# Sample rows turned as whole 128-row tiles, and retention keys in a zero-padded page

## The chip, the cores and the metric

One Trainium2 chip, one of its cores. The metric is device time in microseconds (us) of one execution of the program; lower is better. The engines are TensorE (PE; its weight loads are shown as PEld), VectorE (DVE), ScalarE (ACT), GpSimd (POOL) and the DMA queues that SyncE (SP) issues.

## The reference

Two layers of a hybrid encoder. In each layer every row of x is normalised and projected by `w_in`; three groups of heads work side by side (four retention heads, eight latent-attention heads, four chunk-band heads); their gated outputs are joined and projected by `w_out` onto the residual. It is done for a prompt of 1024 rows and for a sample of 32 rows that have a past (a retention state, 128 cached latent keys, 128 cached band keys). Of the parts that matter here:

```python
def _retention_block(q, k, v, S):               # per head h, dk = dv = 64
    inner = einsum('blhd,bmhd->bhlm', q, k) * dmask
    o = einsum('bhlm,bmhe->blhe', inner, v) + einsum('blhd,bhde->blhe', q, S) * xi
    S_new = gamma ** L * S + einsum('blhd,blhe->bhde', k * zeta, v)
def _dense_attn(q, k, v, bias):                 # the 32 sample rows, against 128 + 32 keys
    return softmax(q k^T * d ** -0.5 + bias) v
```

## The kernel before

The rows are nine tiles: t = 0 to 7 are 128 prompt rows each, t = 8 holds the 32 sample rows (`n = NS`). A projection needs rows turned (features on the partitions), and so do the keys and queries of every score product. A turn is `tr` (line 185, L187 in the trace): a transpose on TensorE against the top left corner of an identity as large as the input has rows, so a tile of 32 rows is turned by a 32x32 identity. All other products go through `mm` (line 180, L181 in the trace). A product of two plain fp32 operands is two MATMUL records in the trace; a turn, and a product of fp32r operands (the split hi and lo parts of projections and latent scores), is one. A MATMUL's form is read as contraction rows * output rows, so `64*128` uses 64 rows of the array and `32*96 32x32` is a turn of 32 rows into 96.

`layer_in` runs the projections in chunks of columns (`pj` banks), a tile at a time, and spawns tasks from their callbacks: `b_task` (latent attention, with `q_task` and `kv_task`), `band_k_task` and `band_task`, `ret_task` (retention), `mla_sample` and `band_sample` for the sample. A task is a generator; a poll between pieces of a projection steps those that are ready. `NEED` and `MOST` say how many of the 60 pages (SBUF tiles of 128x512 fp32) a kind of task may still need, and a task is stepped only if they are free. A scheduler orders the recorded instructions on each engine; each engine then runs its own in that order. After `layer_in` come latent attention over the prompt (`mla`) and the output projections (`out_part`).

`ret_task` (line 928), once per tile and layer: rotate q and k on POOL and DVE, giving `rz` with q heads 0 to 3 and k heads 0 to 3; turn it in four turns of two heads each (`s<-ident,rz`) into one PSUM bank; ACT copies that to `rT`. Each 128-partition slab of `rT` holds two heads, one on partitions 0 to 63 and one on 64 to 127. So the scores are products over 64 partitions each (`s<-rT 64*128`), those of the first and of the second head of a pair into two PSUM banks. Then the state's update (`s<-zk,rz`), decay on DVE (`inn`), the output (`s<-zk,inn` and `s<-S,rT`), its norm, and two turns of the result (`s<-ident,roc`). The PSUM banks of `ret_task` have the tag "s" (three banks), those of the sample attention the tag "ps" (three).

The turns of the sample's 32 rows are `ps<-ident,z` (in `b_task`, line 609, and in `band_sample`), `ps<-ident,kt` and `ps<-ident,zq` (in `mla_sample`, eight in a row for each half of the heads), `ps<-ident,bqs` (`band_sample`), `s<-ident,rz` and `s<-ident,roc` (`ret_task`) and `s<-ident,yres` (`prep`, between the layers). Attention over values works on 64 output rows (`ps<-P,sv 128*64`, `ps<-bs,bv 128*64`) and stays as it is.

Of the kernel before, what the change touches and what calls it, by code (L numbers as in the profile page):

```python
# [20 lines left out]
NS = 32  # L21
# [37 lines left out]
NEED = dict(prep=2, misc=2, b=8, ret=4, bk=2, bq=7, band=14, smp=3, mla=4)  # L59
MOST = dict(prep=1, misc=2, b=4, ret=2, bk=1, bq=7, band=7, smp=3, mla=4)  # L60
# [42 lines left out]
class Kern:  # L103
# [356 lines left out]
    def prep(self, t, xh, hT):  # L460
# [17 lines left out]
        for j in range(2):  # L478
            p = self.bank((4, 128), "prep")
            for i in range(4):  # L480
                self.tr(p[:, i, :n], xn[j][:n, 128 * i:128 * i + 128])
            self.parts(t, j, p[:, :, :n], hT)
# [82 lines left out]
    def unload(self, t, p, W, z=None, raw=False):  # L565

        if z is None:
            z = self.page([W], name="z")
        with self.urgent(URGENT_Z):
# [11 lines left out]
    def b_task(self, l, t, z, raw):  # L581
# [26 lines left out]
        for i in range(3):  # L608
            self.tr(p[:, i, :n], bn[:n, 128 * i:128 * i + 128])
# [64 lines left out]
    def q_task(self, l, t, n, ch, cl):  # L674
        for c in range(2):
            p = self.bank((4, 96), "b")
            self.latent(p, ch, cl, [(k, self.W["u"][2 * k + c]) for k in range(2)])
            zq = self.page([4, 96], name="zq")
            self.unstack(zq[:n], p)
# [25 lines left out]
    def kv_task(self, l, t, n, ch, cl, kr):  # L705
# [3 lines left out]
        for c in range(2):  # L709
            p = self.bank((4, 128), "b")  # L710
            self.latent(p, ch, cl, [(2, self.W["u"][4 + c])])
            kt = self.page([4, 96], name="kt")
            zk = kt[:, :, :64]
# [43 lines left out]
    def mla_sample(self, l):  # L757
        s = self.bank((2, 160))
        for c in range(2):
# [168 lines left out]
    def ret_task(self, l, t, zk, zq):  # L928
# [3 lines left out]
        z = self.page([2, 4, 2, 32], name="rz")  # L932
        tmp = self.page([2, 4, 2, 32], name="rt")
# [66 lines left out]
        oc = self.page([4, 64], name="roc")  # L1000
        self.act(oc[:n], o[:n])
# [8 lines left out]
        for i in range(2):  # L1010
            self.tr(p[:, i, :n], oc[:n, 2 * i:2 * i + 2].rearrange("p h d -> p (h d)"))
# [264 lines left out]
    def band_sample(self, l, zq, r):  # L1276
        A = self.A
        qn = self.page([4, 64], name="bqs")
        self.tt(qn[:NS], zq, r[:NS].unsqueeze(2).to_broadcast([NS, 4, 64]), OP.mult)
# [4 lines left out]
        p = self.bank((2, 192))  # L1284
        for i in range(2):
            self.tr(p[:, i, :128], kc[:, 128 * i:128 * i + 128])
            self.tr(p[:, i, 128:160], self.bks[:NS, 2 * i:2 * i + 2].rearrange("p h d -> p (h d)"))
            self.tr(p[:, i, 160:192], qn[:NS, 2 * i:2 * i + 2].rearrange("p h d -> p (h d)"))
# [3 lines left out]
        self.act(qT, p[:, :, 160:], scale=self.cols[:, 4:5])  # L1292
# [130 lines left out]
    def out_part(self, l, pairs, x_of, y_of, y_cb=None, eng="D", halves=False):  # L1423
# [10 lines left out]
        def ahead(t, cs):  # L1434
# [3 lines left out]
            for c in cs:  # L1438
                ys[c] = self.page([512], name="yres")
                self.load(ys[c][:n], x_of(t)[:, 512 * c:512 * c + 512])  # L1440
# [31 lines left out]
    def layer_in(self, l, hT):  # L1472
# [35 lines left out]
        def cb_ck(t, p):  # L1508
            self.spawn("bk", self.band_k_task(l, t, self.unload(t, p, 256)))
# [187 lines left out]
```

## Time and profile before

| | us |
|---|---|
| median of 3 runs | 1370.53 |
| lowest and highest of them | 1366.14 and 1373.83 |
| the profiled execution | 1364.83 |
| its span (first to last instruction) | 1363.0 |
| PE busy in it | 1313.6 |
| PEld, DVE, ACT, POOL busy | 1204.4, 847.6, 767.0, 462.8 |
| granted TensorE clock, mean | 0.996 |

The span is cut by stage at about 200, 320, 400, 700, 880, 1000 and 1070 us: projections of layer 0, retention with gates (200 to 320), band attention (to 400), latent attention and output (to 700), and the same again for layer 1. PE's busy time counts a MATMUL from its start to its modelled end, some 0.27 us for a small one, while the next may start 0.11 us later; so what a MATMUL costs on PE is read from the distance of starts, not from its length.

### The profile page before, as it was taken

The page shows a single profiled execution, that of the slowest core. Times are in us where ns is not written, and L with a number is a line of the kernel's source. Part 1 is how long each engine was busy: PE and PEld are TensorE (multiplying, and loading weights), DVE is VectorE, ACT ScalarE, POOL GpSimd, SP SyncE. Part 2 cuts the span into 40 slices and gives each one's busy share as a digit, 9 for nine tenths or more (in the row PEclk, how much of TensorE's full clock was granted, in tenths as well). Part 3 has the DMA queues.
Part 4 walks back from the last instruction along what each step waited for, and adds up shares of the span by engine and source line. Part 5 has one row for each costly group of instructions (what it writes and reads, how often), then busy time and mean ns, then how long its engine had stood idle before and what let it go on. Part 6 is the DMA issues. An engine that isn't in the chain of part 4 may idle for free.

```text
span 1363.0 us, 27760 instructions
## 1 busy us (share of the span) xinstructions
PE 1313.6 (96%) x9883; PEld 1204.4 (88%) x9883; DVE 847.6 (62%) x2568; ACT 767.0 (56%) x2177; POOL 462.8 (34%) x686
## 2 busy tenths in 40 slices
PE   7899999999999999989999999999999999999898
PEld 6799999999898888877889999989999988888786
DVE  7656666666768656656563565675675675665543
ACT  7555463355548667666663554533554585775641
POOL 4666766332002113120323576773310031312210
PEclk9899999999999999999999999999999999999999
DMA  7353430121104433233331534301221152333231
GB/s 249 101 159 101 132 110 17 47 84 48 55 24 115 133 119 111 91 97 109 128 118 34 153 111 130 94 23 47 77 67 41 40 162 87 125 96 120 80 127 66
DMA packets 131074, 130.51 MB, mean 96 GB/s; under 512 B 14392, under 2 KB 107256, under 8 KB 130936
## 3 DMA queue, kind: packets, MB, share of 16 engines
q1 hardware_dynamic: 130360, 127.69, 30.3%
q8 instruction: 78, 1.28, 0.4%
q10 hardware_dynamic: 576, 1.05, 0.2%
q14 instruction: 60, 0.49, 0.1%
HBM read 84.48 MB, written 45.79 MB: 96 GB/s over the span
## 4 chain that ended last, share of the span: by engine, by line
PE 75%; DMA 5%; POOL 5%; DVE 5%; ACT 4%; issue 2%; SPq 0%; ACTq 0%; DVEq 0%; POOLq 0%
PE pj L181 42%; PE s L181 12%; PE ps L181 9%; PE ps L187 8%; POOL rs L246 3%; PE pj L187 2%; DMA raw<-in_w_in 1%; PE s L187 1%; ACT P L191 1%; DVE st L218 1%; DMA qd<-zq 1%; DMA kd<-kt 1%; ACT whi L191 1%; POOL ms L207 1%; DMA raw<-in_w_out 1%
## 5 line engine op out<-in xcount | busy, mean ns | idle before, releaser
L181 PE MATMUL pj<-whi,H 128*128 128x256 f32 (+1 forms) x1792 | 369.2, 297 | 11.0 <-ACT H L191 6.8
L181 PEld LDWEIGHTS pj<-whi,H 128*128 128x128 f32 x1792 | 293.1, 191 | 16.6 <-ACT H L191 7.1
L181 PE MATMUL pj<-wlo,H 128*128 128x256 f32 (+1 forms) x896 | 264.6, 296 | 0.6 <-DVE wlo L214 0.6
L181 PE MATMUL pj<-H,whi 128*128 128x384 f32 (+1 forms) x768 | 192.0, 329 | 0.1
L181 PEld LDWEIGHTS pj<-wlo,H 128*128 128x128 f32 x896 | 171.3, 191 | 3.0 <-DVE wlo L214 1.0
L246 POOL TENSOR_TENSOR rs<-ms,nhalf 128x4 f32<-128x4 f32 (+4 forms) x141 | 166.7, 1183 | 8.8
L199 POOL TENSOR_TENSOR mlo<-mix,mhi 128x256 fp32r<-128x256 f32 x96 | 68.9, 738 | 290.6 <-ACT mhi L191 183.1
L181 PE MATMUL s<-H 96*128 96x384 f32 (+3 forms) x576 | 140.2, 360 | 9.9 <-ACT P L191 9.9
L199 POOL TENSOR_TENSOR wlo<-raw,whi 128x512 fp32r<-128x512 f32 x32 | 41.3, 1295 | 272.5 <-ACT whi L191 159.6
L181 PEld LDWEIGHTS pj<-H,whi 128*128 128x128 f32 x768 | 132.6, 188 | 1.0 <-issue 0.6
L218 DVE TENSOR_REDUCE st<-s 128x1 f32<-128x384 f32 (+3 forms) x240 | 128.0, 535 | 7.3 <-PE s L181 4.5
L191 ACT ACTIVATE P<-ps 128x384 f32<-128x384 f32 (+2 forms) x192 | 89.2, 488 | 73.1 <-PE ps L187 72.1
L181 PE MATMUL pj<-H,wlo 128*128 128x384 f32 (+1 forms) x384 | 125.4, 328 | 0.0
L207 POOL TENSOR_SCALAR ms<-st 128x4 f32<-128x4 f32 (+6 forms) x166 | 58.3, 351 | 194.6 <-DVE st L218 166.0
L191 ACT ACTIVATE P<-s,st 128x384 f32<-128x384 f32 (+2 forms) x192 | 110.1, 580 | 20.9 <-DVE st L207 18.4
L191 ACT ACTIVATE whi<-raw,cols 128x256 fp32r<-128x256 f32 (+2 forms) x182 | 85.5, 517 | 62.0 <-DMA raw<-in_w_in 44.5
L214 DVE SCALAR_TENSOR_TENSOR wlo<-raw,cols,whi 128x256 fp32r<-128x256 f32 (+2 forms) x184 | 88.7, 515 | 38.4 <-ACT whi L191 27.4
L181 PEld LDWEIGHTS s<-H 96*128 96x128 f32 x576 | 93.1, 189 | 20.9 <-ACT P L191 13.3
L181 PE MATMUL pj<-whi,mhi 128*128 128x512 f32 x256 | 102.8, 401 | 1.0 <-ACT mhi L191 0.4
L181 PE MATMUL pj<-wlo,mhi 128*128 128x512 f32 x256 | 101.1, 395 | 0.0
L181 PE MATMUL pj<-whi,mlo 128*128 128x512 f32 x256 | 100.5, 394 | 0.0
L187 PE MATMUL ps<-ident,P 128*128 128x128 f32 x576 | 87.3, 273 | 6.5 <-ACT P L191 6.5
(253 smaller groups left out, 2809.6 us busy)
## 6 DMA issues: line engine op xcount, KB each, us to landing
raw<-in_w_in SPq DMA_DIRECT2D x80, 256.0 KB, 2.9
raw<-in_w_out SPq DMA_DIRECT2D x32, 256.0 KB, 3.0
yp<-yres SPq DMA_DIRECT2D x32, 256.0 KB, 2.0
yres<-yp SPq DMA_DIRECT2D x32, 256.0 KB, 3.0
qd<-zq SPq DMA_DIRECT2D x32, 192.0 KB, 1.9
kd<-kt SPq DMA_DIRECT2D x32, 192.0 KB, 2.3
bd<-z SPq DMA_DIRECT2D x48, 128.0 KB, 1.8
sk<-kd SPq DMA_DIRECT2D x32, 192.0 KB, 2.6
```

The lines of the kernel that those rows point to most:

```text
L181: self.nc.tensor.matmul(out, lhsT, rhs, start=start, stop=stop)
L187: self.nc.tensor.transpose(out, in_, self.ident[:k, :k])
L191: r = self.nc.scalar.activation(out, in_, func, **kw)
L199: (self.nc.vector if eng == "D" else self.nc.gpsimd).tensor_tensor(out, a, b, op=op)
L207: (self.nc.vector if eng == "D" else self.nc.gpsimd).tensor_scalar(out, a, s1, s2, op0=op0, **kw)
L214: self.nc.vector.scalar_tensor_tensor(out, a, s, b, op0=op0, op1=op1)
L218: self.nc.vector.tensor_reduce(out, in_, axis=AX.X, op=op, negate=negate)
L246: self.nc.gpsimd.tensor_tensor(r[:n], ms[:n], self.nhalf[:n, :w], op=OP.pow)
```

## The change

1. Each turn of a sample tile now takes the whole page of 128 rows and the whole 128x128 identity. Rows 32 to 127 of that page have to be zeros, so the page is set to zero on POOL before the 32 rows are written (`z`, `zq`, `kt`, `rz`, `roc`, `bqs`, `yres`, and `z` of the band's keys). Consumers still read 32 columns of the result. `mla_sample` and `band_sample` use a bank of their own for the turned q.
2. In `ret_task`, for all nine tiles: `rT` keeps the q slabs only; the turned keys go to a new page `kz`, zeroed on POOL, in two ACT copies, one head's 64 partitions into the first half and the other's into the second. The score products then contract over all 128 partitions (zeros meet the other head's queries), and all four land in one PSUM bank instead of two.
3. `NEED` and `MOST` of retention go from 4 and 2 pages to 5 and 3.

```diff
-NEED = dict(prep=2, misc=2, b=8, ret=4, bk=2, bq=7, band=14, smp=3, mla=4)
-MOST = dict(prep=1, misc=2, b=4, ret=2, bk=1, bq=7, band=7, smp=3, mla=4)
+NEED = dict(prep=2, misc=2, b=8, ret=5, bk=2, bq=7, band=14, smp=3, mla=4)
+MOST = dict(prep=1, misc=2, b=4, ret=3, bk=1, bq=7, band=7, smp=3, mla=4)
...
     def unload(self, t, p, W, z=None, raw=False):
...
             z = self.page([W], name="z")
+            if t == 8 and raw:
+                self.memset(z, 0.0, "G")
...
     def mla_sample(self, l):
...
-            p = self.bank((2, 4, 32))
+            p = self.bank((4, 128))
             for i in range(4):
-                self.tr(p[:96, 0, i], self.ks[0][c][:NS, i])
-                self.tr(p[:96, 1, i], self.qs[c][:NS, i])
+                self.tr(p[:96, i], self.ks[0][c][:, i])
             for j in range(2):
-                self.act(kT[j][:96, :, 128:], p[:96, 0, 2 * j:2 * j + 2], scale=self.cols[:96, 1:2])
-            self.act(qT[:96], p[:96, 1], scale=self.cols[:96, 0:1])
+                self.act(kT[j][:96, :, 128:], p[:96, 2 * j:2 * j + 2, :NS], scale=self.cols[:96, 1:2])
+            p = self.bank((4, 128))
+            for i in range(4):
+                self.tr(p[:96, i], self.qs[c][:, i])
+            self.act(qT[:96], p[:96, :, :NS], scale=self.cols[:96, 0:1])
...
     def ret_task(self, l, t, zk, zq):
...
         z = self.page([2, 4, 2, 32], name="rz")
+        if t == 8:
+            self.memset(z, 0.0, "G")
...
         p = self.bank((4, 128), "ret")
         for i in range(4):
-            self.tr(p[:, i, :n], rx[:n, 2 * i:2 * i + 2].rearrange("p h d -> p (h d)"))
-        rT = self.page([4, 128], name="rT")
-        self.act(rT[:, :, :n], p[:, :, :n])
-        yield
-        s = [self.bank((2, n), "ret") for _ in range(2)]
+            self.tr(p[:, i], rx[:, 2 * i:2 * i + 2].rearrange("p h d -> p (h d)"))
+        rT = self.page([2, 128], name="rT")
+        kz = self.page([2, 2, 128], name="kz")
+        self.memset(kz, 0.0, "G")
+        self.act(rT[:, :, :n], p[:, :2, :n])
         for i in range(2):
             r = slice(64 * i, 64 * i + 64)
+            self.act(kz[r, i, :, :n], p[r, 2:, :n])
+        yield
+        s = self.bank((2, 2, n), "ret")
+        for i in range(2):
             for pr in range(2):
-                self.mm(s[i][:n, pr], rT[r, 2 + pr, :n], rT[r, pr, :n], True, True)
+                self.mm(s[:n, i, pr], kz[:, i, pr, :n], rT[:, pr, :n], True, True)
+        self.free(kz)
...
-                self.stt(inn[:n, i, pr], s[i][:n, pr], GAM[2 * pr + i] ** -n, self.tri[:n, :n], OP.mult, OP.mult)
+                self.stt(inn[:n, i, pr], s[:n, i, pr], GAM[2 * pr + i] ** -n, self.tri[:n, :n], OP.mult, OP.mult)
```

The other turns (in `prep`, `b_task`, the result's turn in `ret_task`, `band_sample`) change in the same way, each with its memset where the page isn't zeroed already.

The built programs have 8774 products and turns each. Three places of PE's order follow; `pj` are projections, which fill the space between tasks.

First, PE at the retention scores of the fourth tile of layer 0. Before:

```order
L181 MATMUL pj_3658<-H_94,wlo_3319 128x288
L181 MATMUL pj_3658<-H_94,whi_3318 128x288
L181 MATMUL pj_3658<-H_95,whi_3318 128x288
L181 MATMUL s_3668<-rT_3633 128x128 x2
L181 MATMUL s_3669<-rT_3633 128x128 x2
L181 MATMUL s_3674<-zk_2261,rz_3520 128x128 x2
L181 MATMUL pj_3658<-H_94,wlo_3319 128x288
```

With the change:

```order
L181 MATMUL pj_3679<-H_94,whi_3260 128x288
L181 MATMUL pj_3679<-H_95,whi_3260 128x288
L181 MATMUL s_3689<-rT_3623,kz_3624 128x128 x4
L181 MATMUL s_3694<-zk_2263,rz_3501 128x128 x2
L187 MATMUL s_3702<-ident,rz_3587 128x128 x4
L181 MATMUL pj_3679<-H_94,wlo_3261 128x288
```

The four score products stand together as before, now with `kz` as an operand and one bank, and the next tile's turns follow at once.

Second, PE in layer 1 at the first half of the latent sample's turns (`kt` 96x128 of cached keys, then keys and queries of the 32 rows). Before:

```order
L181 MATMUL pj_12459<-wlo_12185,H_94 128x256
L181 MATMUL pj_12459<-whi_12184,H_95 128x256
L187 MATMUL ps_12512<-ident,kt_12251 96x128 x4
L187 MATMUL ps_12519<-ident,kt_12339 96x32
L187 MATMUL ps_12519<-ident,zq_12132 96x32
L187 MATMUL ps_12519<-ident,kt_12339 96x32
L187 MATMUL ps_12519<-ident,zq_12132 96x32
L187 MATMUL ps_12519<-ident,kt_12339 96x32
L187 MATMUL ps_12519<-ident,zq_12132 96x32
L187 MATMUL ps_12519<-ident,kt_12339 96x32
L187 MATMUL ps_12519<-ident,zq_12132 96x32
L181 MATMUL pj_12492<-whi_12160,H_94 128x256
```

With the change:

```order
L187 MATMUL s_12650<-ident,rz_12481 128x128 x4
L187 MATMUL ps_12668<-ident,kt_12295 96x128 x4
L187 MATMUL ps_12675<-ident,kt_12412 96x128 x4
L187 MATMUL ps_12682<-ident,zq_12175 96x128 x4
L181 MATMUL s_12688<-rT_12604,kz_12605 128x128 x4
L181 MATMUL s_12693<-zk_11478,rz_12446 128x128 x2
```

The turns are grouped by operand, retention's stand beside them, and they come 150 rows after the product that makes the sample's keys (row 4861 of PE's list to row 5011) where before it was 80 (row 4872 to row 4952).

Third, PE in layer 0 where the band sample's softmax comes back (`ps<-bkT,bqT` are its scores, `bPs` the probabilities that are turned). Before:

```order
L181 MATMUL ps_4859<-bkT_4811,bqT_4812 32x160 x4
L187 MATMUL ps_4889<-ident,bs_4831 128x128 x2
L187 MATMUL ps_4934<-ident,bPA_4856 128x128
L181 MATMUL pj_5069<-H_95,whi_4334 128x288
L181 MATMUL pj_5069<-H_94,wlo_4335 128x288
L187 MATMUL ps_4937<-ident,bs_4749 128x128 x2
L187 MATMUL ps_4941<-ident,bPs_4866 128x128 x2
L181 MATMUL ps_4988<-bPA_4593,bv_4125 64x128
```

With the change:

```order
L181 MATMUL pj_5146<-H_95,whi_4972 128x384
L181 MATMUL pj_5146<-H_94,wlo_4973 128x384
L187 MATMUL ps_4928<-ident,bs_4875 128x128 x2
L187 MATMUL ps_4932<-ident,bPs_4861 128x128 x2
L187 MATMUL ps_4978<-ident,bPA_4900 128x128
L181 MATMUL s_5174<-bk_4258,bqh_4357 128x256
L181 MATMUL s_5174<-bk_4258,bql_4358 128x256
L187 MATMUL ps_4981<-ident,bs_4792 128x128 x2
L181 MATMUL ps_5008<-bPTs_4935,bkc_4761 64x32
```

Between the scores and the turn of `bPs` there were five rows; now there are 53 (the scores are row 2059, the turn row 2113), most of them projections, and the product that uses the turned probabilities comes five matmuls after the turn.

## Rows read from the trace of the kernel before

**Rows 1.** The page, part 1: busy us of each engine, share, instructions.

```profile
PE 1313.6 (96%) x9883; PEld 1204.4 (88%) x9883; DVE 847.6 (62%) x2568; ACT 767.0 (56%) x2177; POOL 462.8 (34%) x686
```

**Rows 2.** Windows of the retention stages: stretch, length, busy PE PEld DVE ACT POOL, clock, DMA.

```profile
200.00:320.00 120.00, 119.48 (x992) 114.03 (x991) 80.14 (x233) 53.49 (x145) 53.30 (x72) 1.00 0.16 47
...
880.00:1000.00 120.00, 118.73 (x970) 112.18 (x969) 78.61 (x229) 53.15 (x150) 56.33 (x73) 1.00 0.19 53
```

**Rows 3.** Waits of PE by releaser: total us, times, longest us.

```profile
PE ps L187 <- DVE st L226: 1.9, 1, 1.9
...
PE ps L187 <- DVE kt L199: 1.2, 1, 1.2
...
PE s L187 <- DVE inn L214: 0.5, 1, 0.5
```

**Rows 4.** Timeline of PE at one tile's scores: start us, length us, instruction, count.

```profile
219.13 0.28 PE L181 MATMUL pj<-whi,H 128*128 128x256 f32 x1
219.34 0.72 PE L181 MATMUL s<-rT 64*128 64x128 f32 x8
220.00 0.71 PE L181 MATMUL s<-zk,rz 128*128 128x128 f32 x4
220.46 0.36 PE L181 MATMUL pj<-whi,H 128*128 128x256 f32 x1
220.66 0.28 PE L181 MATMUL pj<-wlo,H 128*128 128x256 f32 x1
```

**Rows 5.** The same where a tile's scores are split in two runs.

```profile
912.35 0.28 PE L181 MATMUL pj<-wlo,stk 128*96 128x256 f32 x1
912.47 0.28 PE L181 MATMUL pj<-whi,stk 128*96 128x256 f32 x1
912.68 0.71 PE L181 MATMUL s<-rT 64*128 64x128 f32 x4
913.32 0.36 PE L181 MATMUL pj<-wlo,stk 128*96 128x256 f32 x1
913.51 0.28 PE L181 MATMUL pj<-whi,stk 128*96 128x256 f32 x1
```

**Rows 6.** The same at a run of eight sample turns (first row: four full, one small).

```profile
217.02 0.80 PE L187 MATMUL ps<-ident,kt 128*96 128x128 f32 x5
...
218.09 0.39 PE L181 MATMUL pj<-whi,H 128*128 128x256 f32 x1
218.31 0.28 PE L181 MATMUL pj<-wlo,H 128*128 128x256 f32 x1
```

**Rows 7.** The same at three sample turns, a run of two and a single one.

```profile
183.31 0.40 PE L181 MATMUL pj<-whi,H 128*128 128x256 f32 x2
...
183.88 0.38 PE L181 MATMUL pj<-wlo,H 128*128 128x256 f32 x1
...
184.37 0.50 PE L181 MATMUL pj<-whi,H 128*128 128x256 f32 x2
184.71 0.27 PE L181 MATMUL pj<-wlo,H 128*128 128x256 f32 x1
```

**Rows 8.** The same in `band_sample`; between these: two runs of two turns, bkc, bql.

```profile
338.73 0.27 PE L187 MATMUL ps<-ident,bkc 128*128 128x128 f32 x1
...
339.89 0.28 PE L181 MATMUL s<-bk,bqh 128*128 128x256 f32 x1
```

**Rows 9.** Groups of ACT by form: busy us, mean ns, idle us before by releaser.

```profile
L191 ACT ACTIVATE bk<-ps 64x256 fp32r<-64x256 f32 x32 | 11.3, 375 | 12.2 <-DVE bk L199 8.0 <-PE ps L187 4.0
...
L191 ACT ACTIVATE rT<-s 128x512 f32<-128x512 f32 x16 | 9.6, 599 | 8.9 <-PE s L187 8.8
```

**Rows 10.** Groups of POOL by form: a memset of a page.

```profile
L230 POOL MEMSET vp<- 128x512 f32 x2 | 1.1, 526 | 0.1
```

**Rows 11.** Timeline of ACT: the sample's turned copy, layer 1.

```profile
979.94 0.28 ACT L191 ACTIVATE rT<-s 128x128 f32<-128x128 f32 x1
```

**Rows 12.** Timeline of PE: the sample's scores, layer 1.

```profile
980.88 0.32 PE L181 MATMUL s<-rT 64*32 64x32 f32 x8
```

More of the change, by code (lines that the diff above doesn't have):

```diff
@@ L480, in prep @@
             for i in range(4):
-                self.tr(p[:, i, :n], xn[j][:n, 128 * i:128 * i + 128])
+                self.tr(p[:, i], xn[j][:, 128 * i:128 * i + 128])
             self.parts(t, j, p[:, :, :n], hT)
@@ L608, in b_task @@
         for i in range(3):
-            self.tr(p[:, i, :n], bn[:n, 128 * i:128 * i + 128])
+            self.tr(p[:, i], bn[:, 128 * i:128 * i + 128])
         ch, cl = self.page([3, 128], F32R, name="ch"), self.page([3, 128], F32R, name="cl") if t < 8 else None
@@ L678, in q_task @@
             zq = self.page([4, 96], name="zq")
+            if t == 8:
+                self.memset(zq, 0.0, "G")
             self.unstack(zq[:n], p)
@@ L712, in kv_task @@
             kt = self.page([4, 96], name="kt")
+            if t == 8:
+                self.memset(kt, 0.0, "G")
             zk = kt[:, :, :64]
@@ L932, in ret_task @@
         z = self.page([2, 4, 2, 32], name="rz")
+        if t == 8:
+            self.memset(z, 0.0, "G")
         tmp = self.page([2, 4, 2, 32], name="rt")
@@ L1000, in ret_task @@
         oc = self.page([4, 64], name="roc")
+        if t == 8:
+            self.memset(oc, 0.0, "G")
         self.act(oc[:n], o[:n])
@@ L1010, in ret_task @@
         for i in range(2):
-            self.tr(p[:, i, :n], oc[:n, 2 * i:2 * i + 2].rearrange("p h d -> p (h d)"))
+            self.tr(p[:, i], oc[:, 2 * i:2 * i + 2].rearrange("p h d -> p (h d)"))
         self.free(oc)
@@ L1278, in band_sample @@
         qn = self.page([4, 64], name="bqs")
+        self.memset(qn, 0.0, "G")
         self.tt(qn[:NS], zq, r[:NS].unsqueeze(2).to_broadcast([NS, 4, 64]), OP.mult)
@@ L1283, in band_sample @@
         yield
-        p = self.bank((2, 192))
+        p = self.bank((2, 256))
         for i in range(2):
             self.tr(p[:, i, :128], kc[:, 128 * i:128 * i + 128])
-            self.tr(p[:, i, 128:160], self.bks[:NS, 2 * i:2 * i + 2].rearrange("p h d -> p (h d)"))
-            self.tr(p[:, i, 160:192], qn[:NS, 2 * i:2 * i + 2].rearrange("p h d -> p (h d)"))
+            self.tr(p[:, i, 128:], self.bks[:, 2 * i:2 * i + 2].rearrange("p h d -> p (h d)"))
         kT = self.page([2, 160], name="bkT")
@@ L1291, in band_sample @@
         self.act(kT, p[:, :, :160])
-        self.act(qT, p[:, :, 160:], scale=self.cols[:, 4:5])
+        p = self.bank((2, 128))
+        for i in range(2):
+            self.tr(p[:, i], qn[:, 2 * i:2 * i + 2].rearrange("p h d -> p (h d)"))
+        self.act(qT, p[:, :, :NS], scale=self.cols[:, 4:5])
         yield
@@ L1439, in ahead @@
                 ys[c] = self.page([512], name="yres")
+                if t == 8 and y_cb is not None:
+                    self.memset(ys[c], 0.0, "G")
                 self.load(ys[c][:n], x_of(t)[:, 512 * c:512 * c + 512])
@@ L1508, in cb_ck @@
         def cb_ck(t, p):
-            self.spawn("bk", self.band_k_task(l, t, self.unload(t, p, 256)))
+            z = self.page([256], name="z")
+            if t == 8:
+                self.memset(z, 0.0, "G")
+            self.spawn("bk", self.band_k_task(l, t, self.unload(t, p, 256, z=z)))
         def cb_cv(t, p):
```

## The prediction

> **What bounds the kernel now.** First the page's first part: PE is busy for 1313.6 of 1363.0 us [rows 1], and no other engine comes near. Then the windows of the two stages in which most of the change lies: PE is busy for 119.48 of 120 us and for 118.73 of 120 us, at a granted clock of 1.00, which is the 2.4 GHz level, while POOL and ACT are busy for less than half of them [rows 2]. So there TensorE's own stream of instructions sets the time, and a change to it counts at full price; work on ACT and POOL costs only where PE comes to wait for it. Third the waits: in these stages PE waits for little. Three waits bear on instructions that the change touches or moves: 1.9 us before the turn of the band sample's probabilities, 1.2 us before the sample keys' turn, 0.5 us before a turn of `rz` that found no bank [rows 3]. Last the timeline of PE round the instructions that are replaced, because what a run of small products costs is seen only in the starts of its neighbours.
>
> **The scores of the prompt tiles.** An ordinary 128x256 projection starts 0.12 us after the one before (912.35 to 912.47 [rows 5]). A full-array fp32 record costs 0.115 us: four of `zk,rz` from 220.00 to 220.46 [rows 4]. The eight score records of a tile now: from the last ordinary start, 219.13, to the second one after, 220.66, are 1.53 us; taking off 0.12 for the projection at 219.13, 0.12 for that at 220.46 and 0.46 for the `zk,rz` leaves 0.83 us for the eight with the entry and the exit of the run [rows 4]. One tile's scores are split; a run of four costs 912.47 to 913.51, 1.04, less twice 0.12, that is 0.80 us [rows 5]. Of the 17 runs of this form 15 are whole and two are halves of that tile. After, a tile has eight full records: 0.92 us. So 15 x 0.09 = +1.35, and for the split tile 0.92 - 1.60 = -0.7: **+0.65 us**. In words: products of half the array run two at a time, and what that saves is just what entering and leaving the run costs. A full-size record could cost a little less than 0.115 (the four include an entry), so the bounds are -0.5 and +1.4.
>
> The Trainium skill (TensorE: Matmul & The Clock Gate, Part 3) says that products on different row groups run concurrently, which speaks against this edit. With nothing else to pay, eight would pass in the time of four, 0.46 us, and the edit would cost 16 x 0.46 = 7.4 us; a run of eight at 0.83 beside a run of four at 0.80 agrees that the second four are nearly free, but the run as a whole isn't cheap.
>
> **The sample's turns.** A full turn I price at 0.115 too. Eight in a row with the latent keys: 217.02 to 218.31 is 1.29; less four full turns (0.46) and one projection (0.12) leaves 0.71, against 0.92 after: +0.21, four such runs, +0.85 [rows 6]. Three in `b_task`: 183.31 to 184.71 is 1.40, less five ordinary projections (0.60) leaves 0.80 against 0.35: -0.45; in layer 1 the three are one run, and with the price of a run of two (next) I take -0.1 [rows 7]. `band_sample`: 338.73 to 339.89 is 1.16, less two full turns and one band product (0.35) leaves 0.81 for two runs of two, against 0.46: -0.35 a layer, -0.7 [rows 8]. The result's turns of retention are a run of two a layer: half of that, -0.35 in all. Runs of four (`rz`) and the run of eight in `prep` lie between a run of two that gains 0.18 and one of eight that loses 0.21: zero. **Sum -0.75 us**, bounds -2 and +0.5. The sample's scores go from 64 rows and 32 outputs to 128 and 32; they still need a run of their own: zero, within 0.5.
>
> **Runs of other forms.** The order built for the changed kernel has 67 runs of 64-output value products where the old one has 64, because tasks fall differently between them. An additional run costs at most what a run of four pays over its stream, 0.80 - 0.46 = 0.34 [rows 5]: **+1.0 us**, with zero as the other bound.
>
> **Waits.** The turn of `bPs` came five rows after the scores on which its softmax rests; now 53 rows, mostly projections of over 0.12 us each, lie between. So its 1.9 us go. The sample's keys are turned 150 rows after their product, before it was 80 with 1.2 us of waiting: these go too [rows 3]. The 0.5 at `rz` I leave, since the new order puts the next tile's turns right behind the scores. **-3.1 us**. Against that, the product after the turn of `bPs` now follows five matmuls later, about 0.6 us, while an ACT copy of that size takes about 0.38 [rows 9] and can't begin before the turn ends; I allow +0.3.
>
> **ACT and POOL.** Instead of one copy of 0.599 us, ACT makes three of some 0.375 for each prompt tile [rows 9]; that is the price of a 64x256 copy and I take it for the 128x256 one too. That adds 0.53 us to the way from turn to scores, and 16 x 0.53 = 8.5 us to an engine that has over 60 us free in each of these windows [rows 2]. What hides it is the projections between turn and scores: the tightest pair before ends its copy at 980.22 and starts its product at 980.88, 0.66 us of room [rows 11, 12]. POOL zeroes 18 pages for `kz` at 0.526 us [rows 10] and 20 smaller or equal ones for the sample: at most 38 x 0.526 = 20 us of 1363, of which about 9.5 fall into the two windows where POOL has over 60 us free. Nothing on POOL need wait for the turn, so the zeroing can be done ahead. Cost: zero if cover holds (the second rival prices its loss). The page quota of retention could hold back other tasks; but in the built order the latent attention and output stages stand at the same rows as before to within some tens, and the weight loads keep their places among the loads, so I price it at zero too.
>
> **Sum:** +0.65 - 0.75 + 1.0 - 3.1 + 0.3 = -1.9 us. The profiled execution of 1364.83 us would become 1363. Since that is 5.7 us under the median of the runs shown, I put the change on the median: 1370.5 - 1.9, about **1368.5 us**. A change of 0.5%, 6.9 us, is about what a measurement of this kernel can tell from none, so this counts as no change. The bounds together: at the low end -3.0 for scores and turns, nothing for the value products and -3.6 if the wait at `rz` goes too, that is -6.6; at the high end +2.4 for scores and turns, +1.0 for the value products and no gain from the waits, that is +3.4.
>
> **Rival 1, faster: changing the array's form costs more than its neighbours show.** The built order has 168 runs of equal form where the old one has 231: 63 changes fewer. If each run that goes were worth the 0.34 us that a run of four pays over its stream [rows 5], and full products cost nothing beyond that stream, half of 63 x 0.34 = -10.7 us would be found on top of the waits: 1370.5 - 10.7 - 3.1 = 1357 us. For it: nearly all the odd runs are paid for by PE in stages where it never rests. Against it: the pairs in a run of eight are nearly free now, and lose that.
>
> The Trainium skill (TensorEngine Tiling (Array Packing), Key Properties) says that changing the tiling mode drains the engine, which is this rival's mechanism; 219.13 to 219.34 at the entry of a run, where 0.12 is ordinary, agrees with a drain and gives its size [rows 4].
>
> **Rival 2, slower: the longer way from turn to scores.** A score product needs `rz` turned, then the zeroing of `kz` on POOL and three copies on ACT in place of one. PE runs its list in order, so when `kz` is late every projection behind it waits too. The way grows by 0.53 us on ACT, and by up to 0.53 more if the zeroing stands behind other POOL work; the tightest room is 0.66. If all 18 tiles were as tight, each would wait 0.4 us, 7.4 us in all, and with the other direct terms (+0.9) and none of the old waits' gain the time is 1370.5 + 8.3 = 1379 us. It decides as soon as the way grows by more than the projections placed between. Against it: only the sample's pair is that tight in the rows; a prompt tile's scores start some us after their copy.
>
> **Rival 3, no gain from the waits.** The order moves, and as much new waiting arises as goes, in the band or value products that now fall elsewhere: the direct terms alone, +0.9, or 1371.5 us. PE's waits on this stage's tasks are a lottery of some us, and nothing in the rows excludes it.
>
> **How the numbers follow.** Forecast (1368.5, with the bounds round it 1364 to 1374): 0.52. Rival 3: 0.24. Rival 1: 0.13. Rival 2: 0.11. The forecast's lower edge barely reaches 0.5%, so faster by over 0.5%: 0.15; within: 0.74; slower: 0.11. The range leaves the far halves of rivals 1 and 2 out: 1358 to 1378 us.
>
> **What would show it.** In the profile after: runs of `s<-rT,kz 128*128` whose eight records are 0.11 to 0.12 us apart with no step at entry or exit (scores right); eight full turns where the 32x32 ones were; PE's waits without the 1.9 us on `st` and the 1.2 us on `kt` (waits right); no wait of PE on ACT `kz` or POOL `kz` (rival 2 wrong); POOL's busy time up by under 20 us and ACT's by some 9. If PE's busy time falls by about 10 us, rival 1 is right. What would make it wrong altogether is a stage that the order hardly moves, above all latent attention, coming out slower or faster.

## The result: 0.8% slower, and the profile after

| | before | after |
|---|---|---|
| median of the runs, us | 1370.23 | 1381.34 |
| lowest and highest | 1366.14 and 1375.93 | 1375.43 and 1385.49 |
| the profiled execution | 1364.83 | 1378.19 |
| its span | 1363.0 | 1376.4 |

The ratio is 1.0078, with a 95% interval of 1.0052 to 1.0105. The forecast was no change, 1368.5 us in 1358 to 1378; the median is 3.3 us above the upper end. The profiled pair is 13.4 us apart.

The page's first part of the kernel after, beside [rows 1]:

```profile
PE 1320.6 (96%) x9883; PEld 1214.4 (88%) x9883; DVE 852.4 (62%) x2570; ACT 777.3 (56%) x2213; POOL 474.7 (34%) x724
```

ACT has 10.3 us more and POOL 11.9 us, where some 9 and under 20 were priced. The retention stages, beside [rows 2] (stretch, length, busy time of PE, PEld, DVE, ACT and POOL, clock, DMA share, GB/s):

```profile
200.00:320.00 120.00, 119.70 (x992) 116.91 (x992) 80.43 (x229) 58.71 (x164) 61.74 (x88) 1.00 0.16 47
880.00:1000.00 120.00, 118.53 (x971) 115.40 (x970) 79.90 (x219) 56.25 (x164) 60.59 (x86) 1.00 0.19 53
```

PE hardly rests there, as before. The scores themselves, beside [rows 4]: eight full records from 236.28 to 237.17, 0.89 us, with no step at entry or exit. From the projection ahead of them to the second one behind (236.16 to 237.74) are 1.58 us, where the same stretch took 1.53.

```profile
236.16 0.28 PE L181 MATMUL pj<-whi,H 128*128 128x256 f32 x1
236.28 1.05 PE L181 MATMUL s<-rT,kz 128*128 128x128 f32 x8
237.17 0.61 PE L181 MATMUL s<-zk,rz 128*128 128x128 f32 x4
```

The time is lost elsewhere. PE's waits over the whole run, the largest that are new or have grown, beside [rows 3], whose three are gone (5.6 us on `whi` in the first 70 us are left out: they stand where 6.2 us on `H` stood before):

```profile
PE pj L181 <- ACT z L191: 5.1, 6, 1.5
...
PE s L181 <- DVE bs L199: 3.7, 6, 1.0
PE ps L187 <- ACT bPA L191: 3.0, 5, 0.8
PE pj L181 <- DVE z L199: 2.0, 1, 2.0
PE pj L181 <- DVE th L214: 1.3, 1, 1.3
PE ps L187 <- DVE mix L199: 1.1, 1, 1.1
```

Before, the wait for ACT on `z` (the unloading of a projection) was 3.0 us. `bs` and `bPA` are the scores and probabilities of the band attention, `th` and `mix` the gates and what they gate; the change touches none of these four.

**A ledger of PE.** For every MATMUL I took the distance from its start to the next start and compared it with the median distance of the same product in the kernel before. *Own* is the distance behind the changed products and turns (up to 0.3 us; what is longer is a stop), and the excess where the array's form changes. A *stop* is otherwise an excess of over 0.15 us without a change of form. *Half clock* is the part that a distance owes to a granted clock of 0.5. What is left is the ordinary work and small excesses.

| us | before | after | difference |
|---|---|---|---|
| ordinary work at its median | 1224.4 | 1224.3 | -0.1 |
| own | 60.3 | 61.7 | +1.4 |
| stops | 48.2 | 59.7 | +11.5 |
| half clock | 4.8 | 6.2 | +1.4 |
| small excesses | 14.1 | 13.7 | -0.4 |
| first to last start | 1351.7 | 1365.6 | +13.9 |

The lines are rounded. How the medians are taken moves the differences of *own* and of the stops by 1 to 1.5 us. So the parts that the prediction worked out one by one cost about +1.4 us, where it had +0.9, and the loss is stops. By stage, stops and half clock together:

| stage, us | what runs | before | after |
|---|---|---|---|
| 0 to 70 | start | 15.5 | 15.7 |
| 70 to 125 | end of the first projection, layer 0 | 2.0 | 5.9 |
| 125 to 200 | projections, layer 0 | 0.0 | 0.2 |
| 200 to 400 | retention, first band blocks | 2.7 | 1.0 |
| 400 to 450 | last band blocks, layer 0 | 5.3 | 9.5 |
| 450 to 700 | latent attention, output | 14.7 | 14.2 |
| 700 to 1000 | projections, retention, layer 1 | 3.3 | 3.3 |
| 1000 to 1150 | band, layer 1 | 2.1 | 6.9 |
| 1150 to 1310 | latent attention, layer 1 | 7.4 | 9.2 |

**Stop 1, the sample tile's unloading.** The kernel after, POOL, ACT, DVE and PE about 75 us:

```profile
73.31 0.45 POOL L230 MEMSET z<- 128x416 f32 x1
...
74.36 0.91 ACT L191 ACTIVATE whi<-raw,cols 128x256 fp32r<-128x256 f32 x2 [0.64 <-DMA raw<-in_w_in]
75.30 0.51 ACT L191 ACTIVATE z<-pj 32x416 f32<-32x416 f32 x1
...
75.83 0.58 DVE L199 TENSOR_TENSOR z<-pj,z 32x416 f32<-32x416 f32 x1 [1.31 <-ACT z L191]
...
76.47 0.39 PE L181 MATMUL pj<-whi,H 128*128 128x256 f32 x1 [1.97 <-DVE z L199]
```

`z` is zeroed before it is written, so ACT's list has the unloading behind two weight splits (`whi`) that wait for a DMA. The projection's bank is free only when DVE has added the second half, and PE's next projection waits 1.97 us for it, where it waited 0.55 us before. A second new wait of this stage is a prompt tile's, with nothing zeroed; there too ACT's list has the unloading behind two weight splits that wait for a DMA:

```profile
105.37 0.39 PE L181 MATMUL pj<-whi,H 128*128 128x256 f32 x1 [1.08 <-ACT z L191]
```

**Stop 2, the band blocks.** PE in layer 0, one block of scores before:

```profile
407.12 0.29 PE L181 MATMUL pj<-H,wlo 128*128 128x288 f32 x1
407.25 0.43 PE L181 MATMUL pj<-H,whi 128*128 128x288 f32 x2
...
407.58 0.27 PE L181 MATMUL s<-bk,bql 128*128 128x128 f32 x1
407.69 0.35 PE L181 MATMUL pj<-H,wlo 128*128 128x288 f32 x1
407.88 0.43 PE L181 MATMUL pj<-H,whi 128*128 128x288 f32 x2
408.14 0.29 PE L181 MATMUL pj<-H,wlo 128*128 128x288 f32 x1
408.27 0.35 PE L181 MATMUL s<-bk,bqh 128*128 128x256 f32 x1
...
408.81 0.49 PE L187 MATMUL ps<-ident,bPA 128*128 128x128 f32 x3
...
410.27 0.33 PE L181 MATMUL s<-bk,bqh 128*128 128x128 f32 x1 [0.52 <-DVE bs L199]
...
411.26 0.55 PE L187 MATMUL ps<-ident,bPA 128*128 128x128 f32 x3 [0.27 <-ACT bPA L191]
```

And the same block after:

```profile
408.79 0.43 PE L181 MATMUL pj<-H,whi 128*128 128x288 f32 x2
409.06 0.29 PE L181 MATMUL pj<-H,wlo 128*128 128x288 f32 x1
...
410.66 0.39 PE L181 MATMUL s<-bk,bqh 128*128 128x256 f32 x1 [0.65 <-DVE bs L199]
...
411.97 0.55 PE L187 MATMUL ps<-ident,bPA 128*128 128x128 f32 x3 [0.58 <-ACT bPA L191]
...
413.48 0.33 PE L181 MATMUL s<-bk,bqh 128*128 128x128 f32 x1 [0.52 <-DVE bs L199]
...
414.80 0.55 PE L187 MATMUL ps<-ident,bPA 128*128 128x128 f32 x3 [0.59 <-ACT bPA L191]
```

A band score is read by DVE, goes through an exponential on ACT and comes back to PE as a turn. What PE does meanwhile is gate projections. Before, seven of these stood between the scores of this block, and two waits came to 0.79 us; after, three, and four waits come to 2.34 us. The other gate projections still run, but where nobody waits. In layer 1 (1000 to 1150 us, +4.8 us) PE's longest waits after are 1.3 us on `th`, 1.0 on `bs`, 0.8 on `bPA`, and 0.8 on ACT's `H`, which is no part of the band: the same kind of loss, but not of the scores alone.

**A wait can be paid twice.** Windows of the kernel after round 443 us (the number ahead of the last two is the granted clock):

```profile
437.00:442.90 5.90, 3.19 (x23) 2.28 (x22) 5.86 (x16) 5.90 (x18) 2.74 (x4) 1.00 0.38 108
442.90:446.30 3.40, 3.40 (x19) 3.04 (x19) 3.04 (x10) 2.87 (x9) 1.05 (x1) 0.50 0.03 5
446.30:450.00 3.70, 3.70 (x47) 3.08 (x43) 3.20 (x11) 1.25 (x5) 2.18 (x4) 1.00 0.42 103
```

PE was busy 3.19 of 5.90 us, no single wait over 1.2 us; then it has 3.4 us at 0.50, the 1.2 GHz level, and starts 19 MATMULs where the next 3.7 us hold 47. The kernel before has a stretch like it from 437 us on; the one after has two others, behind stop 1 (77.6 us) and at 1286 us. (Both have one more in the start stage, from 41.0 and 43.5 us on.) Not each wait brings one: `turns_only`, a run of the next section, has the wait of stop 1 too, 1.99 us up to 77.84, and keeps its clock,

```profile
77.80:81.00 3.20, 3.16 (x26) 3.17 (x27) 1.74 (x5) 2.45 (x13) 2.59 (x5) 1.00 0.36 123
```

and the 1.9 us for `st` [rows 3] left the clock of the kernel before at 1.00. The Trainium skill (TensorE: Matmul & The Clock Gate, Why this matters for your kernels) warns that idle gaps between bursts of matmuls bring the clock down; the trace agrees, and shows it for gaps shorter than that page speaks of, though not for each of them. In 69 runs of the kernel before the time rises by 0.93 us for each 0.001 of mean granted clock that is lacking (least squares); the mean clock was 0.9926 in these and 0.9907 in the nine runs after, so, as an estimate from this slope, some 1.8 us of the loss is clock.

### The profile page after: what moved, and what is told of

Same layout as the page of the kernel before. It is cut to its first block, busy times and chain, and to the rows that moved or that the text cites. A ratio compares the mean times of both kernels' runs of the same rounds, so it can differ in the third digit from the quotient of the medians.

```text
span 1376.4 us, 27848 instructions
## 1 busy us (share of the span) xinstructions
PE 1320.6 (96%) x9883; PEld 1214.4 (88%) x9883; DVE 852.4 (62%) x2570; ACT 777.3 (56%) x2213; POOL 474.7 (34%) x724
## 4 chain that ended last, share of the span: by engine, by line
PE 79%; DVE 5%; DMA 4%; ACT 4%; POOL 2%; issue 2%; SPq 0%; ACTq 0%; POOLq 0%; DVEq 0%
PE pj L181 45%; PE s L181 12%; PE ps L181 10%; PE ps L187 8%; DMA raw<-in_w_in 2%; PE pj L187 2%; PE s L187 1%; ACT P L191 1%; POOL rs L246 1%; DVE st L218 1%; DMA raw<-in_w_out 1%; DVE rz L199 1%; ACT whi L191 1%; DMA qd<-zq 1%; DVE rp L199 1%
## 5 line engine op out<-in xcount | busy, mean ns | idle before, releaser
L207 POOL TENSOR_SCALAR ms<-st 128x4 f32<-128x4 f32 (+6 forms) x166 | 55.5, 334 | 157.6 <-DVE st L218 129.3
```

The source lines that it names most:

```text
L207: (self.nc.vector if eng == "D" else self.nc.gpsimd).tensor_scalar(out, a, s1, s2, op0=op0, **kw)
```

## The experiments

**Theory A**: the changed instructions cost some 1 us, the loss is new waits because the order moved. **Theory B**: it is the added work on POOL and ACT. **Theory C**: the sample turns alone. The quota was settled by building: the kernel before with `NEED` and `MOST` of retention at 5 and 3 and nothing else gives the same program, with the same rows in the same order on all engines, so by itself it costs nothing.

Ratios are against runs of the kernel before beside them. The last four columns are stops and half clock of the profiled execution by stage, as in the ledger.

| run | median us | ratio, 95% interval | 70-125 | 200-400 | 400-450 | 1000-1150 |
|---|---|---|---|---|---|---|
| before | | 1 | 2.0 | 2.7 | 5.3 | 2.1 |
| after | 1381.34 | 1.0078 (1.0052-1.0105) | 5.9 | 1.0 | 9.5 | 6.9 |
| ret_only | 1377.88 | 1.0059 (1.0038-1.0079) | 1.6 | 1.8 | 8.0 | 6.7 |
| turns_only | 1384.07 | 1.0101 (1.0069-1.0132) | 3.0 | 2.9 | 9.8 | 11.2 |
| gap160 | 1374.79 | 1.0041 (1.0023-1.0059) | 0.8 | 7.5 | 4.3 | 2.3 |
| tr62 | 1381.99 | 1.0086 (1.0058-1.0114) | 2.0 | 6.3 | 4.8 | 9.6 |
| dummy_c | 1376.70 | 1.0048 (1.0027-1.0068) | 0.9 | 3.5 | 4.3 | 2.8 |
| z_below | 1383.92 | 1.0106 (1.0074-1.0139) | 2.5 | 1.9 | 10.7 | 8.6 |
| after_gap | 1379.75 | 1.0087 (1.0058-1.0116) | 5.1 | 1.0 | 11.5 | 6.9 |
| after_tr62 | 1380.55 | 1.0093 (1.0063-1.0123) | 4.2 | 0.5 | 10.2 | 7.2 |
| before_notick | 1373.35 | 1.0049 (1.0030-1.0067) | 1.3 | 11.3 | 3.8 | 2.4 |
| after_notick | 1368.07 | 0.9999 (0.9983-1.0015) | 2.9 | 5.4 | 2.4 | 2.1 |
| notick_z | 1365.24 | 0.9975 (0.9961-0.9990) | 1.5 | 3.5 | 3.7 | 4.1 |
| notick_z2 | 1362.44 | 0.9962 (0.9945-0.9978) | 1.5 | 4.1 | 4.1 | 3.8 |

### The two halves of the change

`ret_only` is parts 2 and 3 of the change with the old turns, `turns_only` is part 1 with the old scores and quota. Both are cut out of the kernel after:

```diff
 # ret_only, against after: this turn and all others of part 1 as before, without their memsets
-            self.tr(p[:, i], rx[:, 2 * i:2 * i + 2].rearrange("p h d -> p (h d)"))
+            self.tr(p[:, i, :n], rx[:n, 2 * i:2 * i + 2].rearrange("p h d -> p (h d)"))
 # turns_only, against after: no kz, rT with all four slabs, two banks
-                self.mm(s[:n, i, pr], kz[:, i, pr, :n], rT[:, pr, :n], True, True)
+                self.mm(s[i][:n, pr], rT[r, 2 + pr, :n], rT[r, pr, :n], True, True)
```

> Only the retention scores change (the page kz with its zeroing on POOL, two copies more on ACT, one bank, the page quota 5 and 3); the sample rows are turned 32 at a time as before. Theory A (the added and replaced instructions cost next to nothing, the loss is new waits of PE because the order round the band attention moved): the score runs themselves cost about +0.7 us, the waits at the unloading of the sample tile between 70 and 125 us are those of the kernel before (2 us of stops over 150 ns), and the time is between 0 and +8 us, by what happens to the stops of the band stages (400 to 450 and 1000 to 1075 us). Theory B (the work added on POOL and ACT is itself what PE waits for): +4 to +8 us, lying in the retention stages 200 to 320 and 880 to 1000 us, with PE waiting on kz. Theory C (the sample turns alone cost it): within 2 us of before.

> Only the turns of the sample rows change (whole tiles, zeroed pages); retention scores on 64 rows and the quota 4 and 2 as before. Theory A: the turns cost about -0.8 us, the zeroing of z ahead of the sample tile's unloading costs some 2 to 2.5 us of stops between 70 and 125 us, and the rest is by what happens to the stops of the band stages: 0 to +9 us in all. Theory B (POOL and ACT work): the zeroing is 20 of 38 memsets and no copies, so about +2 to +4 us. Theory C (the sample turns alone cost it): +9 to +13 us, all of the loss of the full change.

Both are slower, by 0.59% (8 us) and 1.01% (14 us); together they would make 22 us, while the whole change makes 11. Costs that don't add up speak against B, which gives each instruction its price, and `ret_only` alone puts C out. In `ret_only` PE doesn't wait on `kz`, 70 to 400 us has 1.3 us less of stops than before, and the loss is in the two band stages, which run nothing of retention. `turns_only` missed A's range (0 to 9 us) and lies near the upper end of C's (9 to 13).

### Orders moved with no instruction changed

```diff
 # gap160, against before
-GAP = 150
+GAP = 170
 # tr62, against before
-        self.tick("P", 60)
+        self.tick("P", 62)
```

> The kernel before with not one instruction more or less: only the planner's constant for the pause between two steps of a task is 170 instead of 150, which moves instructions from row 1066 of PE's list on. Theory A (an order that was tuned for its constants loses by any move of this size): slower by 2 to 10 us, with more stops of PE over 150 ns in the band stages or in latent attention. Theory B (the added work costs, the order doesn't): within 2 us of before.

> The kernel before with not one instruction more or less: only the planner counts 62 instead of 60 ns for a turn, which moves instructions from row 2587 of PE's list on (the end of layer 0's band attention). Theory A: slower by 2 to 8 us, the stages up to 400 us unchanged. Theory B: within 2 us of before.

The first constant is the pause that the planner leaves between two steps of a task, the second its estimate for a turn. Both kernels do exactly the work of the kernel before, and are 0.41% and 0.86% slower; B is out as the only cause. In `tr62` the waits of PE in layer 1's band, 1020 to 1040 us, where the kernel before has none:

```profile
PE ps L187 <- DVE st L207: 2.1, 1, 2.1
PE s L181 <- DVE st L207: 1.0, 2, 0.5
```

and windows there, with the clock's answer:

```profile
1025.00:1031.30 6.30, 3.18 (x24) 1.94 (x22) 4.91 (x17) 2.12 (x7) 0.00 (x0) 1.00 0.31 83
1031.30:1038.10 6.80, 6.38 (x41) 5.12 (x43) 4.91 (x22) 5.68 (x21) 0.00 (x0) 0.50 0.32 80
```

Part of what I expected of `tr62` failed: the 12 us lie above the 2 to 8 that A had, and 200 to 400 us was not unchanged, since a half-clock stretch of 6.8 us fell behind the old wait for `st`, which the kernel before also has, at full clock.

### The added work without the change

```diff
 # dummy_c, against before, in ret_task
         self.act(rT[:, :, :n], p[:, :, :n])
+        for _ in range(2):
+            self.nc.gpsimd.memset(self.scr, 0.0)
+        m = min(n, 120)
+        for i in range(2):
+            r = slice(64 * i, 64 * i + 64)
+            self.nc.scalar.activation(self.scr[r, :2 * m].rearrange("p (a b) -> p a b", a=2), p[r, 2:, :m], AF.Copy)
```

> The kernel before with the added work of the retention scores, but without their products: in each retention task POOL zeroes a scratch tile twice (240 columns each) and ACT makes two more copies of 64x240 from the bank of the turned rows; nothing reads them. 96 of 100 rows of PE's list stand as before, the rest move a little. Theory A (the order decides, the added work costs next to nothing): -1 to +5 us, with PE never waiting on the scratch copies; what there is lies in stops of the band stages or in clock dips. Theory B (ACT's and POOL's work itself): +6 to +10 us, in the retention stages.

0.48% slower, 6.6 us: above A's range and inside B's. PE never waits on `scr`, but the order moved too, in 4 of 100 rows, so this run alone can't tell them apart. In its ledger *own* is 3.5 us over the kernel before, the most in any run. That is the order: four more prompt tiles than before have their scores in two runs of four, like this one, which was whole before:

```profile
226.96 0.71 PE L181 MATMUL s<-rT 64*128 64x128 f32 x4
227.59 0.39 PE L181 MATMUL pj<-whi,H 128*128 128x256 f32 x1
227.91 0.71 PE L181 MATMUL s<-rT 64*128 64x128 f32 x4
```

A tile so split costs some 0.8 us more. Half clock is 9.7 us over the kernel before; over its ten runs the mean clock is 0.9929, as before, so that profile's clock is not typical. What is left of the 6.6 us has no place in the ledger that would tell A from B, so the run stays inconclusive.

### The zeroing on the unloading's way

```diff
 # z_below, against after, in unload
             if t == 8 and raw:
-                self.memset(z, 0.0, "G")
+                self.memset(z[32:64], 0.0, "G")
+                self.nc.gpsimd.memset(z[64:128], 0.0)
```

> The kernel after, except that in the unloading of the sample tile only rows 32 to 127 of z are zeroed, in two memsets, so that the unloading need not come behind the zeroing; PE's list is 99 of 100 rows the same. Theory A: the wait of PE on DVE z (2.0 us, near 76 us) goes, the stops over 150 ns between 70 and 125 us fall from 4.4 to about 2 us and the dip of the clock behind it (1.5 us) goes with them: 2 to 4 us faster than the kernel after, that is +7 to +10 us against before. Rival: the wait comes from where ACT's list puts the unloading, not from the zeroing, and stays: no change against after.

Its local half came true. ACT now unloads ahead of the weight splits:

```profile
75.27 0.51 ACT L191 ACTIVATE z<-pj 32x416 f32<-32x416 f32 x1
75.86 0.91 ACT L191 ACTIVATE whi<-raw,cols 128x256 fp32r<-128x256 f32 x2
```

PE's wait there is 0.6 us instead of 2.0, and the clock doesn't fall. From 77.6 to 81.0 us, first the kernel after, then `z_below`:

```profile
77.60:81.00 3.40, 3.40 (x18) 3.40 (x17) 0.76 (x2) 1.36 (x10) 3.06 (x5) 0.51 0.50 170
```

```profile
77.60:81.00 3.40, 2.65 (x23) 2.44 (x22) 1.70 (x5) 2.09 (x13) 3.06 (x5) 1.00 0.35 118
```

That is 3.4 us in this stage (5.9 to 2.5): 1.4 of wait, 1.5 of half clock, and 0.5 because the wait at 105.37 us isn't there either, while one of 0.8 us at 80.32 us is new. The total gained nothing, where A had 2 to 4 us. One row in a hundred had moved, and in the profile stops and half clock are 1.7 us more in layer 1's band, 1.2 us more in layer 0's, and 6 us more in latent attention, there by half clock alone. The intervals of the two ratios overlap, so what the whole kernel gets from the edit isn't to be read here.

### The changed kernel in other orders

`after_gap` and `after_tr62` are the two edits of `gap160` and `tr62` on the kernel after.

> The kernel after with not one instruction more or less, the planner's pause between two steps of a task 170 instead of 150. Theory A (the kernel before has a favourable order, the one after an average one): the time moves by 2 to 8 us in either direction, as likely down as up, where the same edit made the kernel before 5.7 us slower. Theory B (the added work costs 10 us whatever the order): within 3 us of the kernel after, +8 to +14 us against before.

> The kernel after with not one instruction more or less, 62 instead of 60 ns counted by the planner for a turn. Theory A: the time moves by 2 to 8 us in either direction, where the same edit made the kernel before 12 us slower; with this and the other edit of the planner's constants the mean of the changed kernels should come within 4 us of the mean of the unchanged ones with the same constants. Theory B: the change costs 10 us with these constants too, so +20 us or more against before.

Neither moved the changed kernel: 0.87% and 0.93% slower than before, where it had 0.78%. A had expected 2 to 8 us either way, and misses here; B had `after_gap` right and `after_tr62` wrong (it wanted 20 us or more). Against the unchanged kernel with the same constants they are 0.46% (6 us) and 0.07% (1 us) slower, 3.6 us in the mean, which is inside A's 4 us. But of the six kernels with sample turns or `kz` so far five lay between 0.78% and 1.06%, and all had 6.7 us or more in layer 1's band. It could still be that the changed instructions cost some 6 us in every order: theory D in the runs that follow.

### The planner's count of the zeroing

The planner keeps a clock for each engine, and a task may go on some time after the latest of them. `memset` counts its time on VectorE's clock (`dtick`) even where it runs on POOL, so the 38 new memsets each hold tasks back by up to 0.6 us. The edit counts them nowhere; all instructions stay:

```diff
 # after_notick against after, before_notick against before
         (self.nc.vector if eng == "D" else self.nc.gpsimd).memset(ap, v)
-        self.dtick(ap)
+        if eng == "D":
+            self.dtick(ap)
```

> The kernel after, all its instructions kept; only the planner no longer counts a memset that runs on POOL against VectorE's clock (each counted up to 0.6 us there, and a task may go on only some time after the latest of the engines' clocks). In the built order more projections stand between the band scores of layer 0 and between their turns than in the kernel after. Theory A (the instructions of the change cost some 1 us, its order costs the rest): stops over 150 ns in the band stages (400 to 450 and 1000 to 1150 us) fall from 14.8 us to 8 or less, and the time is 6 to 13 us below the kernel after, that is -2 to +6 us against before. Theory D (the changed instructions cost some 6 us in every order, as the mean of the orders tried so far has it): +6 to +12 us against before.

> The kernel before with the planner's count alone changed as in after_notick (and no other edit): the partner of after_notick for what the change costs under the same rule of the planner. Theory A: between 0 and +8 us against before (its order is moved away from a favourable one), and within 4 us of after_notick. Theory D: 5 us or more below after_notick.

The changed kernel loses its whole loss: 0.9999 (0.9983 to 1.0015), 11 us below the kernel after by the two ratios, with the same instructions. Its windows of the band stages:

```profile
400.00:450.00 50.00, 47.53 (x440) 45.20 (x438) 36.92 (x128) 34.71 (x103) 8.37 (x10) 1.00 0.31 92
1000.00:1150.00 150.00, 148.50 (x1193) 138.73 (x1192) 101.50 (x352) 95.74 (x289) 16.15 (x21) 1.00 0.27 80
```

beside those of the kernel after,

```profile
400.00:450.00 50.00, 44.11 (x371) 38.66 (x369) 37.26 (x126) 34.73 (x102) 8.81 (x10) 0.97 0.30 85
1000.00:1150.00 150.00, 144.81 (x1142) 133.34 (x1141) 101.28 (x355) 94.04 (x286) 17.16 (x22) 1.00 0.25 73
```

PE starts 440 MATMULs instead of 371 in the first. D is out, since every changed instruction is still there, and so is B. `before_notick` is slower than the kernel before, as A said, so the count is not a plain improvement: it is another order, which happens to suit the changed kernel. There the change is worth -0.50% (0.9999 against 1.0049), about 7 us, more than the 4 us that A allowed; most of it is layer 0's first band blocks (200 to 400 us, 11.3 against 5.4).

### Zeroing off the way, in an order that holds

`notick_z` joins `after_notick` and `z_below`, and 99 of 100 rows of PE are those of `after_notick`. `notick_z2` moves two constants in addition:

```diff
 # notick_z2, against notick_z
-GAPS = dict(bk=100, bq=300, ret=450, band=450)
+GAPS = dict(bk=100, bq=300, ret=450, band=400)
-        self.tick("P", 60)
+        self.tick("P", 56)
```

> As after_notick, and in the unloading of the sample tile only rows 32 to 127 are zeroed, so that the unloading need not come behind the zeroing; PE's list is 99 of 100 rows that of after_notick, which makes the two a pair for this memset alone. Theory A: 1.5 to 3 us faster than after_notick, all of it between 70 and 125 us. If the zeroing is hidden anyway: the same time.

> As notick_z with two constants of the planner moved (the pause of the band tasks 400 instead of 450, 56 instead of 60 ns counted for a turn); 94 of 100 rows of PE's list as in after_notick. Theory A: no instruction differs from notick_z, the time differs by the stops alone, by 0 to 6 us in either direction. If it is below the kernel before, it is a changed kernel that beats it.

The size of the step is what A said (1.5 to 3 us), its place only in part: A had all of it between 70 and 125 us. In `after_notick` PE waits for the unloading,

```profile
78.36 0.38 PE L181 MATMUL pj<-whi,H 128*128 128x256 f32 x1 [1.81 <-ACT z L191]
```

in `notick_z` it hardly does,

```profile
77.25 0.38 PE L181 MATMUL pj<-whi,H 128*128 128x256 f32 x1 [0.46 <-DVE z L199]
```

and the median falls from 1368.07 to 1365.24, 2.8 us, of which 1.4 us lie in this stage's stops; the intervals of the two ratios overlap, so the size of the gain is less sure than its place. `notick_z2` is the fastest of all: 0.9962 (0.9945 to 0.9978), 5 us below the kernel before and some 16 us below the kernel after. So the changed kernel has an order that beats the kernel before. The kernel before was not run with these two constants, so how much of the 5 us is the instructions and how much the order isn't shown.

## Why the prediction was wrong

- **The scores and the sample's turns: right.** It had 0.92 us for eight full records, and 0.89 was measured. Scores, turns and changes of form together cost about +1.4 us (60.3 to 61.7) where +0.9 was forecast; in the other kernels with the whole change *own* lies between 60.5 and 61.5. The Trainium skill (TensorE: Matmul & The Clock Gate, Part 3) tells of concurrent row groups; by these alone the scores would have cost 7.4 us, an estimate of the prediction, and the runs decide against it.
- **The waits that go: right.** Those for `st` (1.9 us), `kt` (1.2 us) and `inn` (0.5 us) [rows 3] are not in the trace after.
- **Rival 1: wrong.** It wanted PE's busy time down by about 10 us; it rose by 7.0 us (1313.6 to 1320.6), and *own*, which holds the changes of form, did not fall.
- **Rival 2: wrong.** (Its 18 waits of 0.4 us are 7.2 us, not 7.4.) PE never waits on `kz`. Its zeroing takes 0.523 us and a copy 0.375 us, as priced, and the copies' longer way is covered.
- **ACT and POOL at zero: the first step that failed.** "Nothing on POOL need wait for the turn" was worked out for the scores alone and then used for all 38 memsets. The one of `z` is on the way of a PSUM bank for which PE waits. `z_below` prices that place at some 3 us in the profile, 1.4 us of wait and 1.5 of half clock.
- **The order at zero: the step that cost most.** In the sum it is the term of the waits, -3.1 + 0.3 us: the old waits went, but stops and half clock together came out +12.9 us in the profiled pair. The quota was indeed free. But the prediction took the built order as harmless because the later stages stood "at the same rows as before to within some tens". Rows say where a stage begins, not what stands between a band score and its turn, and there four gate projections fewer are 1.5 us in one block. Two edits with no instruction changed cost 6 and 12 us; `after_notick` gives back all 11.
- **Rival 3 had the mechanism and not the size.** It let as much new waiting arise as goes. In the profile 2.2 us of stops and half clock went (200 to 400 and 450 to 700 us) and about 15 us came. The bound was no reading: the order before has few stops in layer 1's band (2.1 us from 1000 to 1150), so a move has more to lose there than to gain. The rows for it, PE busy 148.57 of 150 us from 1000 to 1150, were in the trace before:

```profile
1000.00:1150.00 150.00, 148.57 (x1184) 137.82 (x1184) 101.08 (x345) 94.55 (x286) 14.90 (x18) 1.00 0.27 79
```

- **The clock was left out.** No term and no rival had it, though waits can bring it down; by the estimate above it is some 1.8 us here.
- **"What would make it wrong altogether"** named latent attention as the stage that might move. That one stayed in layer 0 (14.7 and 14.2 us of stops and half clock from 450 to 700 us) and lost 1.8 us in layer 1; most of the loss was in the band.

What stays open: what the change costs over many orders. The four pairs with equal constants give +0.78, +0.46, +0.07 and -0.50%, a mean of +0.2% with a scatter of more than twice that; the ledger's own, about +1.4 us or less, agrees with it. Which of the planner's decisions puts the gate projections elsewhere was not traced.

## What to carry to other kernels

Where a planner sets the order and its constants were tuned for one program, price an edit's order apart from its instructions: move a constant that changes no instruction, before and after, and see how far the time goes by itself (here some 20 us between the fastest and the slowest order of nearly equal work). Read a new order at what stands between a producer and the engine that waits for it, not at the row where a stage begins. And ask of each new zeroing whose bank or page waits behind it.

## What the runs showed of the hardware

- After a few short waits PE ran at a granted clock of 0.5 for 3.4 us (twice in the kernel after) or 6.8 us (in `tr62`). No wait ahead of the three places shown was longer than 2.1 us. At 77.6 us of the kernel after this cost 1.5 us on top of a wait of 1.97 us; the same wait in `turns_only`, 1.99 us, and one of 1.81 us in `after_notick` cost nothing more.
- Eight score records of 64 rows in one run took 0.83 us [rows 4], four took 0.80 [rows 5]. So splitting a run of eight in two costs some 0.8 us, which is what `dummy_c` shows (1.80 us from 226.75 to 228.55, one projection of 0.12 included, where the whole run took 0.87).
- On ACT and POOL fewer partitions save nothing. Groups of ACT by form in the kernel after, and of POOL in `notick_z` (busy us, mean ns, idle us before):

```profile
L191 ACT ACTIVATE kz<-s 64x256 f32<-64x256 f32 x32 | 12.0, 375 | 0.3
L191 ACT ACTIVATE rT<-s 128x256 f32<-128x256 f32 x16 | 6.2, 385 | 13.4 <-PE s L187 13.4
```

```profile
L230 POOL MEMSET z<- 64x416 f32 x2 | 0.9, 446 | 0.1
L230 POOL MEMSET z<- 32x416 f32 x2 | 0.9, 439 | 0.1
```

The two copies of 64 partitions together take twice the time of one of 128, and zeroing 32 rows takes as long as 64.
